# A third weight buffer, and two plain blocks instead of three at the start of three of the four channel mixers

## The chip, the cores and the metric

One core of one Trainium2 chip runs the whole program in one launch. The metric is the device time of that launch in microseconds (us), the median of several runs. A difference of under about 0.3% (5.7 us of 1895) cannot be told from no change.

## The reference

A decoder trunk of two layers on 512 tokens with 1024 channels, all in float32. Each layer adds half a channel mixer, a token mixer and another half channel mixer to the residual `h`:

```python
def swiglu(x, w_gate, w_up, w_down):          # 1024 -> 2816 -> 1024
    return (jax.nn.silu(x @ w_gate) * (x @ w_up)) @ w_down
...
    for i in range(DEPTH):
        h = h + 0.5 * swiglu(rmsnorm(h, ffn_norm_a[i]), ...)
        m = rmsnorm(h, mix_norm[i])
        h = h + (mla_mixer if i % 2 == 0 else nsa_mixer)(m, ...)
        h = h + 0.5 * swiglu(rmsnorm(h, ffn_norm_b[i]), ...)
    return rmsnorm(h, final_norm)
```

The token mixer of layer 0 ("MLA") is latent attention with 16 heads. That of layer 1 ("NSA") has 16 heads in 4 groups and three branches: over compressed blocks, over chosen blocks and over a window.

## The kernel before

The four channel mixers (`ffn`, `idx` 0 to 3) and the two token mixers (`mla`, `nsa`) run in the order ffn 0, mla, ffn 1, ffn 2, nsa, ffn 3. Nothing but their order in the program separates them: a scheduler in the build fixes each engine's instruction order from the code's dependences and its own costs, and each engine then runs its list in order. So work of the next stage is mixed into the end of the one before wherever buffers allow it.

Every matmul of a projection is done three times (high part by high part, high by low, low by high). Each weight slab therefore arrives raw from memory (tile `wr`, two buffers, 512 KB for a block's gate or up weights), ScalarE (ACT) copies its high part into a tile `w`, and VectorE (DVE), or in the attention loops GpSimd (POOL, switched by `lo_pool`), subtracts to get the low part. `wtiles` hands out the `w` tiles in turn from two buffers.

A channel mixer has 22 blocks of 128 hidden channels. Two ways of computing a block's gate and up projections stand beside each other:

- `plain`: 48 matmuls of 256 columns for the gate (`pg`) and 48 for the up projection (`pu`), straight from the normalised input parts `x`. It needs nothing prepared but the weight splits. The first `PLAIN = 3` blocks of every mixer are of this kind.
- seven `product`s of 12 matmuls each (Strassen-Winograd), 84 matmuls, into banks `px`, `pq` and `pg`. They need sums of input parts, made once per mixer by four calls of `combine` (tiles `y`, `u`, `four`), and sums of weight parts, made for every block by `wsums` (tiles `rg` or `wr`, `ru`, `s1`, split into `w`, `wh`, `wl`). Between the products ACT copies a bank that a later product goes on writing (`pg<-px`, `uq<-pq`, `uq<-px`).

While the plain blocks run, the norm's column is made: the last squares are added (`late`, `sumsq`), summed by four small matmuls (`pc`), and twelve small DVE instructions take the reciprocal root (`rsqrt`, tiles `small`). Four more matmuls spread it (`pb`), ACT copies it (`row`), and only then are the plain blocks gated (`tg`, then `tu`, then the parts `ah` and `al` of the activation). In the order that the code gives, `pb` stands between the gate and the up projection of the last plain block. From the fourth block on, down projections of the preceding three blocks (`unit`: eight per three blocks, weights `wdr`, `wd`, bank `pd`) are put behind the products; the last four blocks' down projections come at the end, with weights that used `wslab` and so the `w` tiles.

In `mla`, `query` splits each head's query; the low part is made on POOL (`pool=True`), as is that of each pair's output (`ol`). In `nsa`, the attention loop carries projections of later groups (`pp`, `pv`) in pieces between its tiles, with slabs from `wslab`.

Of the kernel before, what the change touches and what calls it, by code (L numbers as in the profile page):

```python
# [18 lines left out]
P = 128  # L19
S = 512  # L20
D = 1024
KC = D // P
FF = 2816
NF = FF // P
EPS = 1e-6
NEG = -1e30
H = 16
# [19 lines left out]
LASTK = 4  # L47
HS = S // 2
KP = KC // 2
PLAIN = 3  # L50
PAD = 16
TILES = 24
XC = P + 2
NG = 3
# [8 lines left out]
class Kern:  # L63
# [61 lines left out]

    def wtiles(self, kind="x"):

        t = self.first or self.wp.tile([P, 2048 + 3 * PAD], F32R, tag=f"w{self.nw % 2}", name="w")
        self.nw, self.first = self.nw + 1, None
        o, d = {"x": (0, 0), "act": (3 * PAD, 0), "half": (PAD, 2 * PAD)}[kind]  # L130
        return t[:, o : o + 1024], t[:, o + d + 1024 : o + d + 2048]
# [139 lines left out]
            nc.vector.tensor_tensor(t, t, y, op=ALU.mult)  # L271
            nc.vector.scalar_tensor_tensor(y, t, 1.5, y, op0=ALU.add, op1=ALU.mult)

    def norm_col(self, n, s2, pool=False):

        nc = self.nc
        pc = self.bank("o", "pc")
        for i in range(4):
            nc.tensor.matmul(pc[:, i : i + 1], s2[:, i * P : (i + 1) * P], f32v(self.ones)[:, 0:1], start=True, stop=True)
        return self.rsqrt_col(pc[:, 0:4], n, pool)  # L280

    def rsqrt_col(self, s, n, pool=False):
        v, t, col = self.vtc[:, 0:4], self.vtc[:, 4:8], self.vtc[:, 8:12]
# [25 lines left out]
    def wsums(self, idx, f):  # L309


        nc, fp, w_gu = self.nc, self.fp, self.a["w_gu"]
        if f == PLAIN:

            rg = fp.tile([P, 1024], F32, tag="fr", bufs=3, name="rg")
        else:
            rg = self.wp.tile([P, 1024], F32, tag="wr", bufs=2, name="wr")
        nc.sync.dma_start(rg, w_gu[idx, f, 0])
        ru = fp.tile([P, 1024], F32, tag="fr", bufs=3, name="ru")
        nc.sync.dma_start(ru, w_gu[idx, f, 1])  # L320
        s1 = fp.tile([P, S], F32, tag="s1", bufs=1, name="s1")
        g0, g1, u0, u1 = rg[:, :S], rg[:, S:], ru[:, :S], ru[:, S:]

        def split(src, pool, tag, bufs):
            n = src.shape[1]
# [12 lines left out]
        w[1], w[2] = split(rg, self.wp, None, 2)  # L338
        nc.vector.tensor_tensor(s1, u0, u1, op=ALU.add)
        nc.vector.tensor_tensor(u0, u0, g0, op=ALU.add)  # L340
        w[7], w[4] = split(ru, fp, ("fh", "fl"), 3)
        nc.vector.tensor_tensor(g0, g0, s1, op=ALU.add)
        nc.vector.tensor_tensor(g1, g1, g0, op=ALU.add)
        w[6], w[3] = split(rg, fp, ("fh", "fl"), 3)
        w[5], = split(s1, fp, ("sh", "sl"), 2)
        return w
# [22 lines left out]
    def ffn(self, idx, gain_next, ap, tp):  # L369
        nc, a = self.nc, self.a  # L370
        self.scr, self.fp = (tp, "sq", 1), tp
        ah, al, ht, row = {}, {}, [], None
        tg, tu, units = {}, {}, []

        def gate(f, g):

            t = tg[f] = tp.tile([P, S], F32, tag="tg", bufs=2, name="tg")
            nc.vector.tensor_tensor(t, g, row, op=ALU.mult)
            nc.scalar.activation(t, t, AF.Silu, scale=-1.0)
            nc.vector.tensor_tensor(t, t, row, op=ALU.mult)  # L380
# [3 lines left out]

        def act(f):
            t = tu[f]
            if f < PLAIN:
                t = tu_tile()
                nc.vector.scalar_tensor_tensor(t, tu[f], -1.0, tg[f], op0=ALU.mult, op1=ALU.mult)
            else:  # L390
                nc.vector.tensor_tensor(t, t, tg[f], op=ALU.mult)
            ah[f] = ap.tile([P, S], F32R, tag="act", bufs=4 * NG, name="ah")
            al[f] = ap.tile([P, S], F32R, tag="act", bufs=4 * NG, name="al")
            self.split(t, ah[f], al[f])
# [32 lines left out]
                tokens(t)  # L427


        gates = [self.bank("T", "pg") for _ in range(PLAIN)]  # L430
        for f, g in enumerate(gates):
            u = tu[f] = self.bank(("mm", "S")[f % 2], "pu")
            self.plain(idx, f, 0, g)
            if f == 1 and idx == 0:

                squares(0)
                tokens(3)
                squares(1)
            if f == 2:
                pb = self.norm_bcast(col)  # L440
                row = tp.tile([P, S], F32, tag="row", bufs=1, name="row")
                nc.scalar.activation(row, pb, AF.Copy)
                for e in range(2):
                    gate(e, gates[e])
                    act(e)
            self.plain(idx, f, 1, u)
            if f == 0 and idx:
                for c in self.late:
                    self.sumsq(self.h[c])
                col = self.norm_col(D, self.s2)  # L450
            elif f == 1 and idx == 0:
                squares(2)
                squares(3)
                col = self.rsqrt_col(sums, D)
            elif f == 2:
                gate(f, g)
                act(f)
            for p in (((0,), (1,), (2, 3)) if idx else ((0, 1), (2,), (3,)))[f]:
                self.combine(p)
        t = self.tiny  # L460
        for i, g in enumerate(gates[::-1]):
            nc.scalar.activation(t[:, i + 1 : i + 2], g[:, 0:1], AF.Identity, bias=t[:, i : i + 1])

        tail = PLAIN + (NF - 2 - PLAIN) // NG * NG
        for f in range(PLAIN, NF):
            if f % NG == 0 and f <= tail:
                units = [partial(unit, b0=f - NG, c=c) for c in range(KC)]
                left = NG if f < tail else NF - tail
# [36 lines left out]
        self.norm_begin(gain_next)  # L505
        for c in self.order:
            p = self.mm_bank("pd")
            down(p, self.wslab(a["w_down"][idx, c, :, tail * P :], (NF - tail, P), "act"), tail, NF)
            add(c, p)
            self.norm_chunk(c)  # L510

# [130 lines left out]
    def mla(self, gain_next):  # L642
        nc, tc, a = self.nc, self.tc, self.a
        with ExitStack() as cx:
# [106 lines left out]
            def query(h, w=None):  # L751
                p = self.proj(None, P, cqh, cql, "pq", w or query_slab(h))
                t = tp.tile([P, S], F32, tag="tq", bufs=2, name="tq")
                nc.vector.tensor_tensor(t, p, cst, op=ALU.mult)
                qh, ql = self.qtile(), self.qtile()
                self.split(t, qh, ql, pool=True)
                return qh, ql

            qs, oh, ol, o32 = {}, [], [], [None]
# [15 lines left out]
            def end(h):  # L775
# [5 lines left out]
                if h % 2 == 1:  # L781
                    hi = tp.tile([P, S], F32R, tag="o", bufs=12, name="oh")
                    lo = tp.tile([P, S], F32R, tag="o", bufs=12, name="ol")
                    self.split(o32[0], hi, lo, pool=True)
                    oh.append(hi)
                    ol.append(lo)

# [546 lines left out]
```

## Time and profile before

| | |
|---|---|
| median of 3 runs | 1894.92 us (1894.47 to 1899.17) |
| profiled execution | 1895.84 us, of it 1894.1 us from first to last instruction (the span) |
| TensorE (PE) busy | 1865.5 us, 98% |
| VectorE (DVE) busy | 1527.9 us, 81% |
| ScalarE (ACT) busy | 1088.9 us, 57% |
| GpSimd (POOL) busy | 244.7 us, 13%, all but a little of it in the two attention stages |
| HBM | 179.0 MB read, 96 GB/s over the span |

Stages, by the first matmul of each: ffn 0 from 5.7 us, mla from 346.1, ffn 1 from 560.9, ffn 2 from 898.5, nsa from 1235.8, ffn 3 from 1543.1. In the profile, "L165" is line 165 of the kernel before. A matmul's recorded duration overlaps that of its neighbours, so the pace of TensorE is read from the distance of starts, not from durations.

### The profile page before, as it was taken

The numbers are of one execution on the slowest core, as the hardware profiler recorded it, in microseconds if no ns is written. First come the engines' busy times: TensorE is split into PE (matmuls) and PEld (weight loads), VectorE is DVE, ScalarE is ACT, GpSimd is POOL, SyncE is SP. The second block draws the span as 40 slices with busy tenths as digits, with TensorE's granted clock in tenths as the row PEclk, the third lists the DMA queues.
The fourth block names the chain that finished last, engine by engine and source line by source line (L and its number), as shares of the span: only waits on it lengthen the run. The fifth ranks groups of instructions, "written<-read, shape, count | busy, mean of one in ns | idle before, by whom it ended". The sixth has DMA issues, their size and how long they took to land.

```text
span 1894.1 us, 32916 instructions
## 1 busy us (share of the span) xinstructions
PE 1865.5 (98%) x12504; PEld 1695.8 (90%) x12504; DVE 1527.9 (81%) x2913; ACT 1088.9 (57%) x2024; POOL 244.7 (13%) x334
## 2 busy tenths in 40 slices
PE   8999999999999999999999999999989999999998
PEld 8999999878889999998999999888778889999997
DVE  8988886677778888886898878666978988888885
ACT  8555554478765555554654555436867865555553
POOL 0000000047710000000000000015656600000000
PEclk9999999999999999999999999999999999999999
DMA  6433331311132333322333332143121133333321
GB/s 237 131 101 100 102 100 41 112 53 46 60 132 90 124 101 101 102 79 86 130 124 108 105 105 75 55 141 102 51 71 64 43 115 111 111 107 104 104 77 67
DMA packets 75902, 183.26 MB, mean 97 GB/s; under 512 B 9040, under 2 KB 37072, under 8 KB 75744
## 3 DMA queue, kind: packets, MB, share of 16 engines
q1 hardware_dynamic: 72800, 176.39, 29.4%
q10 hardware_dynamic: 2944, 4.77, 0.7%
q8 instruction: 98, 1.61, 0.4%
q14 instruction: 60, 0.49, 0.1%
HBM read 178.96 MB, written 2.16 MB: 96 GB/s over the span
## 4 chain that ended last, share of the span: by engine, by line
PE 86%; DVE 6%; ACT 4%; POOL 2%; issue 1%; DMA 0%; POOLq 0%; SPq 0%; DVEq 0%; ACTq 0%
PE pd L164 8%; PE pd L165 8%; PE pd L163 8%; PE px L353 5%; PE px L354 5%; PE px L355 5%; PE pg L353 4%; PE pg L354 4%; PE pg L355 4%; PE pq L354 3%; PE pq L353 3%; PE pq L355 3%; PE o L1139 1%; PE po L164 1%; PE po L165 1%; PE po L163 1%
## 5 line engine op out<-in xcount | busy, mean ns | idle before, releaser
L164 PE MATMUL pd<-al,wd 128*128 128x512 f32 x576 | 225.3, 391 | 0.0
L163 PE MATMUL pd<-ah,wd 128*128 128x512 f32 x576 | 224.9, 390 | 0.0
L165 PE MATMUL pd<-ah,wd 128*128 128x512 f32 x576 | 224.6, 390 | 0.0
L172 DVE TENSOR_TENSOR w<-wr,w 128x1024 fp32r<-128x1024 f32 x72 | 88.2, 1224 | 123.9 <-ACT w L171 123.9
L353 PE MATMUL px<-four,wh 128*128 128x256 f32 x608 | 168.8, 278 | 0.6 <-ACT pg L478 0.6
L355 PE MATMUL px<-four,wl 128*128 128x256 f32 x608 | 168.0, 276 | 0.0
L354 PE MATMUL px<-four,wh 128*128 128x256 f32 x608 | 167.9, 276 | 0.0
L353 PE MATMUL pq<-four,wh 128*128 128x256 f32 x608 | 167.8, 276 | 0.0
L354 PE MATMUL pq<-four,wh 128*128 128x256 f32 x608 | 167.8, 276 | 0.0
L355 PE MATMUL pq<-four,wl 128*128 128x256 f32 x608 | 167.8, 276 | 0.0
L144 ACT ACTIVATE w<-wr 128x1024 fp32r<-128x1024 f32 (+5 forms) x120 | 100.7, 845 | 113.7 <-issue 25.7
L171 ACT ACTIVATE wd<-wdr 128x384 fp32r<-128x384 f32 x192 | 99.3, 519 | 98.5 <-ACT wd L171 59.1
L402 DVE SCALAR_TENSOR_TENSOR h<-pd,h 128x512 f32<-128x512 f32 x216 | 147.9, 685 | 6.9 <-PE pd L165 6.8
L165 PEld LDWEIGHTS pd<-ah,wd 128*128 128x128 f32 x576 | 108.2, 188 | 22.8
L163 PEld LDWEIGHTS pd<-ah,wd 128*128 128x128 f32 x576 | 108.1, 188 | 20.5
L164 PEld LDWEIGHTS pd<-al,wd 128*128 128x128 f32 x576 | 108.1, 188 | 19.7
L172 DVE TENSOR_TENSOR wd<-wdr,wd 128x384 fp32r<-128x384 f32 x192 | 106.1, 555 | 16.3 <-ACT wd L171 15.6
L146 DVE TENSOR_TENSOR w<-wr,w 128x1024 fp32r<-128x1024 f32 (+4 forms) x81 | 80.7, 998 | 45.1 <-ACT w L144 44.8
L640 ACT ACTIVATE p<-p,small 128x512 f32<-128x512 f32 (+2 forms) x192 | 106.5, 557 | 17.2 <-DVE small L639 14.2
L353 PEld LDWEIGHTS px<-four,wh 128*128 128x128 f32 x608 | 114.1, 188 | 2.5 <-ACT pg L478 1.9
L353 PEld LDWEIGHTS pq<-four,wh 128*128 128x128 f32 x608 | 114.2, 188 | 0.1
L354 PEld LDWEIGHTS pq<-four,wh 128*128 128x128 f32 x608 | 114.1, 188 | 0.1
(354 smaller groups left out, 6106.3 us busy)
## 6 DMA issues: line engine op xcount, KB each, us to landing
wr<-in_w_gu SPq DMA_DIRECT2D x96, 512.0 KB, 3.3
ru<-in_w_gu SPq DMA_DIRECT2D x76, 512.0 KB, 4.2
wdr<-in_w_down SPq DMA_DIRECT2D x192, 192.0 KB, 2.4
wr<-in_w_down SPq DMA_DIRECT2D x24, 256.0 KB, 2.6
wr<-in_mla_w_o SPq DMA_DIRECT2D x8, 512.0 KB, 3.4
wr<-in_nsa_w_q SPq DMA_DIRECT2D x8, 512.0 KB, 3.3
th<-btab_d SPq DMA_DIRECT2D x16, 256.0 KB, 3.5
wr<-in_nsa_w_o SPq DMA_DIRECT2D x8, 512.0 KB, 3.6
```

Source lines behind the costliest of these rows:

```text
L144: self.copied = nc.scalar.activation(wh[:, m], raw[:, m], AF.Copy)
L146: nc.vector.tensor_tensor(wl[:, m], raw[:, m], f32v(wh[:, m]), op=ALU.subtract)
L163: mm(out, wh, xh, start=first, stop=False)
L164: mm(out, wh, xl, start=False, stop=False)
L165: return mm(out, wl, xh, start=False, stop=last)
L171: nc.scalar.activation(hi, src, AF.Copy)
L172: (nc.gpsimd if pool else nc.vector).tensor_tensor(lo, src, f32v(hi), op=ALU.subtract)
L353: mm(out, wh[:, p], xh, start=first and p == 0, stop=False, skip_group_check=True)
L354: mm(out, wh[:, p], xl, start=False, stop=False, skip_group_check=True)
L355: mm(out, wl[:, p], xh, start=False, stop=last and p == KP - 1, skip_group_check=True)
L402: nc.vector.scalar_tensor_tensor(self.h[c], p, 0.5, self.h[c], op0=ALU.mult, op1=ALU.add)
L640: nc.scalar.activation(p_sb[:, :n], p_sb[:, :n], AF.Exp, bias=nm, scale=-1.0, accum_out=sm)
```

## The change

```diff
-PLAIN = 3
+PLAIN = 3, 2, 2, 2
+URGENT = 400
...
-        t = self.first or self.wp.tile(..., tag=f"w{self.nw % 2}", name="w")
+        t = self.first or self.wp.tile(..., tag=f"w{self.nw % 3}", name="w")
...
-    def norm_col(self, n, s2, pool=False):
+    def norm_col(self, n, s2, urgent=0):
...
-        return self.rsqrt_col(pc[:, 0:4], n, pool)
+        with self.tc.high_priority(urgent) if urgent else nullcontext():
+            return self.rsqrt_col(pc[:, 0:4], n)
...
+        def spread():
+            pb = self.norm_bcast(col)
+            nc.scalar.activation(row, pb, AF.Copy)
+            for e in range(plain - 1):
+                gate(e, gates[e])
+                act(e)
...
-        gates = [self.bank("T", "pg") for _ in range(PLAIN)]
+        gates = [self.bank("T", "pg") for _ in range(plain)]
         for f, g in enumerate(gates):
             u = tu[f] = self.bank(("mm", "S")[f % 2], "pu")
             self.plain(idx, f, 0, g)
+            if f == plain - 1:
+                spread()
...
             if f == 0 and idx:
-                for c in self.late:
-                    self.sumsq(self.h[c])
-                col = self.norm_col(D, self.s2)
+                with self.tc.high_priority(URGENT):
+                    for c in self.late:
+                        self.sumsq(self.h[c])
+                col = self.norm_col(D, self.s2, URGENT)
...
-            for p in (((0,), (1,), (2, 3)) if idx else ((0, 1), (2,), (3,)))[f]:
+            for p in (((0, 1), (2, 3)) if plain == 2 else ((0, 1), (2,), (3,)))[f]:
                 self.combine(p)
...
-            down(p, self.wslab(a["w_down"][idx, c, :, tail * P :], (NF - tail, P), "act"), tail, NF)
+            raw = tp.tile([P, D], F32, tag="fr", bufs=3, name="wdr")[:, : (NF - tail) * P]
+            nc.sync.dma_start(raw, a["w_down"][idx, c, :, tail * P :])
+            w = [... for t in self.sum_tiles(1024)]
+            self.split(raw.rearrange("p (k c) -> p k c", c=P), *w)
+            down(p, w, tail, NF)
...
-                self.split(t, qh, ql, pool=True)          # mla, query
+                self.split(t, qh, ql, pool=h > 1)
...
-                    self.split(o32[0], hi, lo, pool=True) # mla, end of a pair of heads
+                    self.split(o32[0], hi, lo, pool=h + 1 < H)
...
-    nc = bacc.Bacc("TRN2", target_bir_lowering=False, num_devices=1)
+    nc = bacc.Bacc("TRN2", target_bir_lowering=False, num_devices=1, dynamic_dma_scratch_size=1024)
```

In words: ffn 1, 2 and 3 start with two plain blocks, so one more block in each is of the seven-product kind; `w` tiles come from three buffers, and room for the third is taken from a DMA scratch area (16384 bytes per partition before, 1024 after; a `w` tile has 8384); the last four blocks' down weights use the sum tiles; three splits of MLA move from POOL to DVE; the norm column's instructions get priority in the scheduler. The column is `pb`'s input, and `pb` now stands inside the up projection of the second plain block.

TensorE at the start of ffn 1, before:

```order
L365 MATMUL pg<-x,w 128x256
L366 MATMUL pg<-x,w 128x256
L367 MATMUL pg<-x,w 128x256
L291 MATMUL pb<-ident,small 128x128 x4
L365 MATMUL pu<-x,w 128x256
L366 MATMUL pu<-x,w 128x256
```

and in the changed kernel, where 21 of the 48 matmuls of `pu` stand ahead of `pb`:

```order
L367 MATMUL pu<-x,w 128x256
L368 MATMUL pu<-x,w 128x256
L369 MATMUL pu<-x,w 128x256
L293 MATMUL pb<-ident,small 128x128 x4
L367 MATMUL pu<-x,w 128x256
L368 MATMUL pu<-x,w 128x256
```

`pb` moved from behind the third block's gate to 69 matmuls behind the start of the second block (in ffn 2 it is 83, in ffn 3 it is 77).

ScalarE in ffn 1, at the first seven-product block, before (the copies between products are `uq<-pq`, `pg<-px`, `uq<-px`):

```order
L171 ACTIVATE w<-wr 128x1024
L171 ACTIVATE ah<-tu 128x512 x2
L379 ACTIVATE tg<-tg 128x512
L462 ACTIVATE gains<-pg,gains 128x1
L480 ACTIVATE uq<-pq 128x256
L462 ACTIVATE gains<-pg,gains 128x1
L478 ACTIVATE pg<-px 128x256
L462 ACTIVATE gains<-pg,gains 128x1
L482 ACTIVATE uq<-px 128x256
```

and in the changed kernel:

```order
L172 ACTIVATE w<-wr 128x1024
L468 ACTIVATE gains<-pg,gains 128x1
L484 ACTIVATE pg<-px 128x256
L486 ACTIVATE uq<-pq 128x256
L172 ACTIVATE ah<-tu 128x512
L488 ACTIVATE uq<-px 128x256
L172 ACTIVATE ah<-tu 128x512
L172 ACTIVATE wh<-s_6814 128x512
L172 ACTIVATE wh<-ru 128x1024
L491 ACTIVATE pg<-px 128x256
```

One `ah` copy of a plain block now stands between two copies of the first seven-product block, and on TensorE no down projection stands among or behind that block's products, as four `pd` matmuls did before.

GpSimd in the attention loop of NSA, with buffer numbers (a name in the changed kernel counts 42 higher than the same tile before; `w_15652` and `w_15658` are the two slabs of `vals`, that is `w_15694` and `w_15700` after), before:

```order
L1091 TENSOR_SCALAR p_15434<-p_15434,small_76,gat_14124 128x512
L1091 TENSOR_SCALAR p_15457<-p_15457,small_76,gat_14124 128x384
L172 TENSOR_TENSOR ohl_15480<-o32_15260,ohl_15479 128x512
L1091 TENSOR_SCALAR p_15489<-p_15489,small_76,gat_14124 128x384
L150 TENSOR_TENSOR w_15652<-wr_15651,w_15652 128x512 x2
L1091 TENSOR_SCALAR p_15508<-p_15508,small_76,gat_14124 128x512
```

and in the changed kernel:

```order
L1101 TENSOR_SCALAR p_15476<-p_15476,small_76,gat_14166 128x512
L1101 TENSOR_SCALAR p_15499<-p_15499,small_76,gat_14166 128x384
L173 TENSOR_TENSOR ohl_15522<-o32_15302,ohl_15521 128x512
L1101 TENSOR_SCALAR p_15531<-p_15531,small_76,gat_14166 128x384
L151 TENSOR_TENSOR w_15700<-wr_15699,w_15700 128x512 x2
L1101 TENSOR_SCALAR p_15550<-p_15550,small_76,gat_14166 128x512
```

The place of the first `vals` slab now holds the second: the low parts of all slabs of the loop stand one slab earlier.

More of the change, by code (lines that the diff above doesn't have):

```diff
@@ L126, in wtiles @@
     def wtiles(self, kind="x"):
-        t = self.first or self.wp.tile([P, 2048 + 3 * PAD], F32R, tag=f"w{self.nw % 2}", name="w")
+        t = self.first or self.wp.tile([P, 2048 + 3 * PAD], F32R, tag=f"w{self.nw % 3}", name="w")
         self.nw, self.first = self.nw + 1, None
@@ L312, in wsums @@
         nc, fp, w_gu = self.nc, self.fp, self.a["w_gu"]
-        if f == PLAIN:
+        if f == PLAIN[idx]:
             rg = fp.tile([P, 1024], F32, tag="fr", bufs=3, name="rg")
@@ L371, in ffn @@
         self.scr, self.fp = (tp, "sq", 1), tp
-        ah, al, ht, row = {}, {}, [], None
+        ah, al, ht, plain = {}, {}, [], PLAIN[idx]
         tg, tu, units = {}, {}, []
@@ L386, in act @@
             t = tu[f]
-            if f < PLAIN:
+            if f < plain:
                 t = tu_tile()
@@ L427, in ffn @@
                 tokens(t)
-        gates = [self.bank("T", "pg") for _ in range(PLAIN)]
+        def spread():
[4 more added lines that the diff above has]
+                act(e)
+        row = tp.tile([P, S], F32, tag="row", bufs=1, name="row")
+        gates = [self.bank("T", "pg") for _ in range(plain)]
         for f, g in enumerate(gates):
@@ L438, in ffn @@
                 squares(1)
[L439 to L445, printed above, removed]
             self.plain(idx, f, 1, u)
             if f == 0 and idx:
-                for c in self.late:
-                    self.sumsq(self.h[c])
-                col = self.norm_col(D, self.s2)
+                with self.tc.high_priority(URGENT):
+                    for c in self.late:
+                        self.sumsq(self.h[c])
+                col = self.norm_col(D, self.s2, URGENT)
             elif f == 1 and idx == 0:
@@ L454, in ffn @@
                 col = self.rsqrt_col(sums, D)
-            elif f == 2:
+            if f == plain - 1:
                 gate(f, g)
                 act(f)
-            for p in (((0,), (1,), (2, 3)) if idx else ((0, 1), (2,), (3,)))[f]:
+            for p in (((0, 1), (2, 3)) if plain == 2 else ((0, 1), (2,), (3,)))[f]:
                 self.combine(p)
@@ L462, in ffn @@
             nc.scalar.activation(t[:, i + 1 : i + 2], g[:, 0:1], AF.Identity, bias=t[:, i : i + 1])
-        tail = PLAIN + (NF - 2 - PLAIN) // NG * NG
-        for f in range(PLAIN, NF):
+        tail, left = (NF - 2) // NG * NG, 1
+        for f in range(plain, NF):
             if f % NG == 0 and f <= tail:
@@ L507, in ffn @@
             p = self.mm_bank("pd")
-            down(p, self.wslab(a["w_down"][idx, c, :, tail * P :], (NF - tail, P), "act"), tail, NF)
+            raw = tp.tile([P, D], F32, tag="fr", bufs=3, name="wdr")[:, : (NF - tail) * P]
+            nc.sync.dma_start(raw, a["w_down"][idx, c, :, tail * P :])
+            w = [t[:, : (NF - tail) * P].rearrange("p (k c) -> p k c", c=P) for t in self.sum_tiles(1024)]
+            self.split(raw.rearrange("p (k c) -> p k c", c=P), *w)
+            down(p, w, tail, NF)
             add(c, p)
```

## The prediction

> **What bounds the kernel now.** I read the page first (busy times, chain), then the stage windows, then TensorE's waits, and then single stretches of the timeline.
>
> ```profile
> span 1894.1 us, 32916 instructions
> PE 1865.5 (98%) x12504; PEld 1695.8 (90%) x12504; DVE 1527.9 (81%) x2913; ACT 1088.9 (57%) x2024; POOL 244.7 (13%) x334
> PE 86%; DVE 6%; ACT 4%; POOL 2%; issue 1%; DMA 0%; POOLq 0%; SPq 0%; DVEq 0%; ACTq 0%
> ```
>
> TensorE (PE) is 98% busy and carries 86% of the chain that ended last. DMA is no part of that chain (0%), so the smaller DMA scratch, of which no row shows a use, is costed at nothing; were transfers to slow down, this share would show it.
>
> The next rows are windows: start and end, length, then busy time and count of PE, PE weight loads, DVE, ACT, POOL, and last the granted clock, DMA share and GB/s. The first is the whole of ffn 1, the second its opening up to about the fourth block.
>
> ```profile
> 560.80:898.50 337.70, 337.48 (x2429) 315.70 (x2429) 279.46 (x437) 180.21 (x291) 0.00 (x0) 1.00 0.32 101
> 560.80:609.90 49.10, 48.91 (x408) 47.73 (x408) 42.48 (x72) 31.71 (x47) 0.00 (x0) 1.00 0.35 117
> ```
>
> PE is without a break at full clock in a channel mixer: 0.22 us idle in 337.70. So a matmul less is time saved, as long as nothing else becomes late. DVE is the nearest rival: 83% over the stage, 42.48/49.10 = 87% in the opening, and the opening is what the change shortens.
>
> PE's waits of 0.2 us or more that the change can touch (engine, line, releaser: total us, times, longest):
>
> ```profile
> PE ptc L1058 <- POOL e L1053: 4.1, 4, 2.4
> PE pv L164 <- POOL w L150: 1.7, 2, 1.0
> PE pg L353 <- ACT pg L485: 1.2, 3, 0.8
> PE px L353 <- ACT pg L478: 0.6, 3, 0.2
> ```
>
> **T1, matmuls out.** Each of ffn 1, 2, 3 has one plain block (96 matmuls) less and one seven-product block (84) more: 12 less each, 36 in all. The first two rows stand half a plain block apart, the last two a whole seven-product block:
>
> ```profile
> 578.13 0.28 PE L365 MATMUL pu<-x,w 128*128 128x256 f32 x1
> 583.57 0.28 PE L365 MATMUL pg<-x,w 128*128 128x256 f32 x1
> 1200.40 0.28 PE L353 MATMUL px<-x,w 128*128 128x256 f32 x1
> 1209.97 0.39 PE L163 MATMUL pd<-ah,wd 128*128 128x512 f32 x1
> ```
>
> 583.57 - 578.13 = 5.44 us for 48 matmuls, 0.1134 each. A plain block is 10.88, a seven-product block 9.57. Per mixer 10.88 - 9.57 = 1.31, for three 3.93; by count 36 x 0.1134 = 4.08. I take -4.0. On DVE and ACT the swap adds work: three DVE sums and four splits in place of two splits, and three bank copies on ACT. That is covered by PE in the middle of a mixer; in the opening it isn't certain (T4).
>
> **T2, the third weight buffer in the NSA loop.** Four waits of PE are for a slab part that was split late, since the slab before held the buffer:
>
> ```profile
> 1306.88 0.50 PE L165 MATMUL pp<-x,w 128*128 128x512 f32 x1 [0.59 <-POOL w L150]
> 1383.30 0.39 PE L163 MATMUL pv<-w,x 128*128 128x256 f32 x1 [0.71 <-ACT w L144]
> 1384.70 0.38 PE L164 MATMUL pv<-w,x 128*128 128x256 f32 x1 [1.02 <-POOL w L150]
> 1386.41 0.58 PE L164 MATMUL pv<-w,x 128*128 128x256 f32 x1 [0.73 <-POOL w L150]
> ```
>
> The sum is 0.59 + 0.71 + 1.02 + 0.73 = 3.05 us. In the changed order the low parts stand a whole slab earlier on POOL, so all four should go; the matmul after a wait can itself be slower (0.58 in the last row, against 0.28 in T1's first), for which I allow 0.15 each, an estimate of half that difference. I take -3.2; the ends are 0 (waits that only move) and -3.7. What is late next is the wait for `e` on POOL (4.1 us in the waits above, 2.4 its longest): it stands behind the same POOL work as before, so I leave it. A raw slab still has only two `wr` buffers, and a transfer can't start earlier than those come free; the split then waits instead of the matmul.
>
> **T3, three splits from POOL to DVE in MLA.** Two waits of PE are for them. Behind the first two rows stand DVE's time for such a split twice, alone and beside a POOL split; then POOL's own pair, beside that DVE one and in two separate instructions.
>
> ```profile
> 402.56 0.50 PE L165 MATMUL s<-four 128*128 128x512 f32 x1 [0.63 <-POOL four L172]
> 543.70 0.50 PE L164 MATMUL po<-ol,w 128*128 128x512 f32 x1 [0.63 <-POOL ol L172]
> 1386.71 0.69 DVE L929 TENSOR_TENSOR four<-t,four 64x512 fp32r<-64x512 f32 x1
> 1383.80 1.40 DVE L929 TENSOR_TENSOR four<-t,four 64x512 fp32r<-64x512 f32 x1 [1.03 <-ACT four L928]
> 1383.39 2.97 POOL L150 TENSOR_TENSOR w<-wr,w 128x512 fp32r<-128x512 f32 x2
> 1407.09 1.30 POOL L150 TENSOR_TENSOR w<-wr,w 128x512 fp32r<-128x512 f32 x1
> ```
>
> POOL takes 1.30 for 512 columns, DVE 0.69: the split is done 0.6 us sooner, just what PE waited (0.63 twice). With both gone, -1.26; I take -1.2. DVE's three extra instructions, 3 x 0.69 = 2.1 us, lie at the edges of MLA, beside PE work. The ends: -1.8 with what a restart costs, and +1.5 if DVE takes 1.40 as in the fourth row (0.71 more at each of two places, late for PE instead).
>
> That fourth row and the POOL pair of 2.97, against 2 x 1.30, ran at the same time, and both are long. The Trainium skill, page "SBUF — State Buffer", section "Who interferes with whom", says that a DVE operation with two inputs in SBUF and a GpSimd one shut each other out for a whole instruction. The trace agrees for this pair; by that rule, with POOL still splitting the next heads, T3 would come out near its upper end (R4 below) instead of at -1.2.
>
> **T4, the openings of ffn 1, 2, 3.** What goes: the waits of the two last rows of PE's waits above, 1.2 + 0.6 = 1.8 us, which lie at first seven-product blocks. What may come: two things.
>
> *The column.* PE runs its list in order, so if the norm's column is not there when PE reaches `pb`, PE stops.
>
> ```profile
> 560.85 0.28 PE L365 MATMUL pg<-x,w 128*128 128x256 f32 x1
> 572.59 0.36 PE L365 MATMUL pg<-x,w 128*128 128x256 f32 x1
> 568.47 0.68 DVE L340 TENSOR_TENSOR ru<-ru,rg 128x512 f32<-128x512 f32 x1
> 569.07 1.22 DVE L146 TENSOR_TENSOR w<-wr,w 128x1024 fp32r<-128x1024 f32 x1
> 570.21 1.22 DVE L172 TENSOR_TENSOR four<-u,four 128x1024 fp32r<-128x1024 f32 x1
> 571.34 0.42 DVE L238 TENSOR_TENSOR u<-y,u 128x256 f32<-128x256 f32 x1
> 571.68 0.68 DVE L237 TENSOR_TENSOR u<-y 128x512 f32<-128x512 f32 x1
> 577.71 0.15 DVE L272 SCALAR_TENSOR_TENSOR small<-small 128x4 f32<-128x4 f32 x1
> 582.83 0.15 DVE L272 SCALAR_TENSOR_TENSOR small<-small 128x4 f32<-128x4 f32 x1
> 589.01 0.49 PE L291 MATMUL pb<-ident,small 128*128 128x128 f32 x3
> ```
>
> The first block with the column's sums takes 572.59 - 560.85 = 11.74 us. In the new order 69 matmuls follow before `pb` in ffn 1, 83 in ffn 2, 77 in ffn 3: PE is there 11.74 + 69 x 0.1134 = 19.6, 21.2 and 20.5 us after the opening's start. Before, the column ended 582.83 + 0.15 - 560.85 = 22.1 after it, and had until 589.01 (28.2). So it must come 2.5 us sooner. DVE's rows ahead of the column's last instruction in the new order of ffn 1 are 9 of 512 columns, 2 slightly longer squares, 7 of 1024, 8 of 256 and 12 tiny ones. By distances of starts above: 9 x 0.60 + 2 x 0.67 + 7 x 1.14 + 8 x 0.34 + 12 x 0.07 = 18.3 us, from about 1.0 after the start: 19.3, against 19.6. (0.67 is an estimate from the 512-column row; 0.07 is half the tiny ones' 0.15, since they overlap.) For ffn 2 and 3 the same count gives 21.5 and 20.8 against 21.2 and 20.5: 0.3 us late each. Both are closer than a hand count can tell; I take +0.6 for the three.
>
> *The gating.* Once spread, the column goes through ACT and DVE before the plain blocks' `ah` is there:
>
> ```profile
> 590.30 0.60 ACT L442 ACTIVATE row<-pb 128x512 f32<-128x512 f32 x1
> 590.91 1.28 ACT L379 ACT_TABLE_LOAD   x1
> 592.21 1.19 ACT L379 ACTIVATE tg<-tg 128x512 f32<-128x512 f32 x2
> 584.92 1.23 DVE L146 TENSOR_TENSOR w<-wr,w 128x1024 fp32r<-128x1024 f32 x1 [1.94 <-ACT w L144]
> 590.30 1.22 DVE L172 TENSOR_TENSOR w<-rg,w 128x1024 fp32r<-128x1024 f32 x1 [4.16 <-ACT w L171]
> 1601.30 0.53 ACT L171 ACTIVATE wd<-wdr 128x384 fp32r<-128x384 f32 x1 [1.70 <-DMA wdr<-in_w_down]
> 1603.10 0.39 PE L353 MATMUL pg<-x,wh 128*128 128x256 f32 x1 [0.79 <-ACT pg L485]
> ```
>
> From PE's 19.6: `pb` and `row` until 21.0, table load until 22.3, the two `tg` until 23.5, then DVE's products on top of its splits, and `tu` at about 28.8 to 29.3. In ACT's new order one `ah` copy, which needs `tu`, stands between the copies `uq<-pq` and `uq<-px`; `uq<-px` is then done at 29.7, and the product that goes on in that bank could start at 28.9. PE waits about 0.8, in each of three openings: +2.4. Before, `pd` matmuls stood there as cover; now none do, so nothing hides it. DVE had 1.94 + 4.16 us idle in the old opening (rows 584.92 and 590.30); the new block's sums and splits eat that. The ends of T4 are -1.8 (no new wait at all) and +4 (the column 0.5 late and the `ah` stall 1.4 in each). Sum: 2.4 + 0.6 - 1.8 = +1.2.
>
> An example of such a chain is in the last two rows: a `wd` copy on ACT waited 1.70 for its transfer, and PE then waited 0.79 for a bank copy that stood behind it and needed nothing of it. [...]
>
> The tail's down weights (sum tiles in place of `w`), PLAIN's effect on the blocks' numbering and the moves of `combine` cost nothing on PE: same matmuls, and DVE has 17% free over the stage (window of ffn 1). Without that cover the tail's DVE split, four parts of 0.60, would cost at most 2.4 per mixer; no row points to that.
>
> **The sum.** -4.0 - 3.2 - 1.2 + 1.2 = -7.2 us. The profiled execution before took 1895.84 (span 1894.1 and 1.7 around it), 0.92 over the median of 1894.92. So 1888.6 for a profiled run, 1887.7 for the median.
>
> **The rivals.**
>
> R1, the openings become DVE-bound: T4 is at +4 and T3 at 0, so the sum is -4.0 - 3.2 + 4 = -3.2, 1891.7, no change that can be measured. For it speaks DVE's 87% in the opening with a block that needs more DVE work; against it that PE loses only the excess over 1 or 2 us there.
>
> R2, the third buffer only moves the waits: the raw slabs have two buffers still, and POOL does its list in order. T2 is about 0: -4.0 - 1.2 + 1.2 = -4.0, 1890.9, no change. For it speaks the `e` row, which shows POOL late in that loop anyway; against it that the parts stand a slab earlier on POOL.
>
> R3, slower: the column stays as late as it was, and each `pb` stops PE. Without T4 the sum is -8.4; to be slower by over 5.7 us the openings have to lose 14.1, or 4.7 each, so the column must come later than 19.6 + 4.7 = 24.3 after the start. Say 25: 3 x 5.4 = 16.2, and 1894.92 - 8.4 + 16.2 = 1902.7. Against it: it came at 22.1 without any priority (2.5 late, 7.5 for three: 1894.0, still no change). For it: twelve dependent instructions on a DVE that has new sums to make, each of which can be put behind a 1.2 us split; in the trace of ffn 1 the last one ended 5 us after an earlier one (rows 577.71 and 582.83).
>
> R4, DVE and POOL stand in each other's way in MLA: T3 is +1.5, as in the 1.40 row. The sum is -4.0 - 3.2 + 1.5 + 1.2 = -4.5, 1890.4, no change. Against it: one such pair in the rows, and the three splits are at the edges of MLA, where POOL has just lost that work.
>
> R5, better: no new wait in the openings, T4 at -1.8, restarts at their best: -4.1 - 3.7 - 1.8 - 1.8 = -11.4, 1883.5.
>
> **How the numbers follow.** Forecast 0.51, R1 0.18, R2 0.14, R3 0.06, R4 0.04, R5 0.07. A difference of 0.3%, 5.7 us, is about what a measurement of this kernel can tell from no change. The forecast's case has about 0.02 on its upper side that lies within it. Faster by more (below 1889.2): 0.49 + 0.07 of R5 + 0.04 of R2 (waits that go in part) = 0.60. Slower: 0.06. The rest, 0.34, is within. The range leaves out R3 and holds the other cases but for their outer parts, since each rests on hand counts: low 1882 (R5 and 1.5 under it), high 1893.5 (R1 with the column 2 us later in one opening).
>
> **What the profile of the changed kernel would show.** T1: windows of ffn 1 and 2 shorter by 1.3 us each, less what their openings wait. T2: no wait for `w` at `pp` and `pv`; if R2, the same microseconds under another tile. T3: the two 0.63 waits gone, no DVE row of 1.4 in their place. T4: `pb` without a wait, and one wait near 0.8 for `uq` on ACT in each opening. I am wrong if `pb` waits for DVE's `small` by more than 2 us in each opening, if the NSA stage keeps its length, or if another engine's name takes over the waits in the opening.

## The result, and the profile after

The changed kernel takes 1913.87 us (median of 4; 1913.42 to 1916.35), the kernel before, measured beside it, 1895.37: ratio 1.0096, 95% interval 1.0079 to 1.0114. It is 18.5 us slower, where 1887.7 was forecast.

From the changed kernel's page (its span is 1912.5 us):

```profile
PE 1888.3 (99%) x12468; PEld 1720.0 (90%) x12468; DVE 1554.5 (81%) x2940; ACT 1080.0 (56%) x2039; POOL 242.0 (13%) x331
```

The 36 matmuls are gone (12504 to 12468), and still TensorE is busy for 22.8 us more. So it does not wait more; its matmuls have become slower. PE's waits in the changed kernel say the same:

```profile
PE pg L367 <- ACT w L145: 5.8, 1, 5.8
PE ptc L1068 <- POOL e L1063: 3.1, 3, 2.4
PE pb L293 <- DVE small L273: 1.4, 3, 0.7
```

The first row is the start of the program and was there before (5.7). The waits for `w` in NSA have gone, `pb` waits 1.4 us in all (0.65 of it in MLA, about 0.4 in the openings of ffn 1 and of ffn 2). By stage (ffn 0, mla, ffn 1 and 2, nsa, ffn 3), first the kernel before, then the changed one:

```profile
5.74:346.13 340.39, 340.12 (x2420) 317.29 (x2421) 285.11 (x445) 188.68 (x306) 0.00 (x0) 1.00 0.36 115
346.13:560.85 214.72, 210.42 (x1105) 176.17 (x1104) 156.84 (x425) 145.49 (x339) 96.30 (x120) 1.00 0.22 70
560.85:1235.83 674.98, 674.57 (x4857) 631.11 (x4856) 559.61 (x876) 358.89 (x580) 2.04 (x6) 1.00 0.32 101
1235.83:1543.06 307.23, 298.62 (x1654) 251.45 (x1653) 240.45 (x687) 209.93 (x493) 146.11 (x206) 0.99 0.24 74
1543.06:1894.05 350.99, 341.76 (x2473) 319.75 (x2471) 284.55 (x478) 182.98 (x303) 0.00 (x0) 1.00 0.32 104
```

```profile
5.80:351.80 346.00, 345.85 (x2420) 323.74 (x2421) 289.67 (x448) 186.61 (x308) 0.00 (x0) 1.00 0.36 117
351.80:567.59 215.79, 211.38 (x1105) 176.33 (x1104) 159.14 (x426) 144.86 (x339) 91.98 (x117) 1.00 0.20 65
567.59:1255.49 687.90, 686.64 (x4833) 643.10 (x4832) 575.96 (x895) 357.93 (x590) 2.09 (x6) 1.00 0.32 101
1255.49:1557.38 301.89, 297.31 (x1654) 251.42 (x1653) 237.56 (x684) 208.19 (x492) 147.76 (x205) 0.99 0.24 74
1557.38:1912.50 355.12, 347.12 (x2461) 325.42 (x2459) 290.81 (x485) 179.47 (x307) 0.00 (x0) 0.99 0.31 100
```

NSA won 5.3 us. All channel mixers lost: ffn 1 and 2 12.9 us with 24 matmuls less, and ffn 0 5.6 us, although it has the same 2420 matmuls as before. The granted clock (third column from the end) is the same to within 0.01, so a lower clock is not the reason. A seven-product block, which took 9.57 us in the prediction, now takes:

```profile
773.07 0.28 PE L355 MATMUL px<-x,w 128*128 128x256 f32 x1
783.05 0.39 PE L164 MATMUL pd<-ah,wd 128*128 128x512 f32 x1
```

783.05 - 773.07 = 9.98 us for 84 matmuls, 118.8 ns instead of 113.9. And within one plain block, gate and up:

```profile
567.59 0.28 PE L367 MATMUL pg<-x,w 128*128 128x256 f32 x1
573.04 0.28 PE L367 MATMUL pu<-x,w 128*128 128x256 f32 x1
578.75 0.39 PE L280 MATMUL pc<-ones,s 128*128 128x1 f32 x3
```

5.45 us for the gate's 48, 5.71 for the up projection's 48 (113.5 and 119.0 ns each): the same matmuls on the same `x`. Only the weights lie in another buffer, the gate's in the second and the up projection's in the third.

The build gives every tile its byte address in a partition. Cut a partition into lines of 128 bytes; an operand begins in the first half of a line (address modulo 128 under 64) or in the second. (A 256-column operand has 1024 bytes and fills whole lines, so only the place where it begins is meant.) A `w` tile has 8384 bytes, which is 65.5 times 128. A third one therefore moves the beginning of all that lies behind it from one half of a line to the other (addresses modulo 128):

| | `x`, `four` | `w` buffers | all behind `w` (sums' `wh`, `wl`; `ah`, `al`, `wd`) |
|---|---|---|---|
| before | 0 mod 128 | 0, 0 | 64 |
| changed | 0 | 0, 0, 64 | 0 |
| changed, 64 bytes more behind `w1` | 0 | 0, 0, 0 | 64 |

The parts of a `w` tile used for a mixer's blocks begin 64 bytes into it (`PAD`). So before, the 256-column matmuls read moving data that begins in the one half, while weights that begin in the other half were loaded. Counted over the built programs, moving data and the weights of the following matmul begin in the same half for 122 of the 7864 matmuls of 256 columns before, for 5940 of 7828 in the changed kernel. For the up projection above they do, since the third `w` buffer begins at 64; for the gate they don't.

### The profile page after: what moved, and what is told of

It is laid out like the page before. It is cut to its first block, busy times and chain, and to the rows that moved or that the text cites. A ratio compares the mean times of both kernels' runs of the same rounds, so it can differ in the third digit from the quotient of the medians.

```text
span 1912.5 us, 32778 instructions
## 1 busy us (share of the span) xinstructions
PE 1888.3 (99%) x12468; PEld 1720.0 (90%) x12468; DVE 1554.5 (81%) x2940; ACT 1080.0 (56%) x2039; POOL 242.0 (13%) x331
## 4 chain that ended last, share of the span: by engine, by line
PE 90%; DVE 4%; ACT 3%; issue 1%; DMA 1%; POOL 1%; POOLq 0%; SPq 0%; DVEq 0%; ACTq 0%
PE pd L165 8%; PE pd L166 8%; PE pd L164 8%; PE px L355 6%; PE px L357 6%; PE px L356 6%; PE pg L355 4%; PE pg L357 4%; PE pg L356 4%; PE pq L357 4%; PE pq L355 4%; PE pq L356 4%; PE po L164 2%; PE o L1149 2%; PE po L165 2%; PE po L166 2%
## 5 line engine op out<-in xcount | busy, mean ns | idle before, releaser
L355 PE MATMUL px<-four,wh 128*128 128x256 f32 x632 | 178.8, 283 | 0.6 <-ACT pg L484 0.6
L357 PE MATMUL px<-four,wl 128*128 128x256 f32 x632 | 178.0, 282 | 0.0
L356 PE MATMUL px<-four,wh 128*128 128x256 f32 x632 | 177.9, 281 | 0.0
L357 PE MATMUL pq<-four,wl 128*128 128x256 f32 x632 | 177.7, 281 | 0.0
L355 PE MATMUL pq<-four,wh 128*128 128x256 f32 x632 | 177.7, 281 | 0.0
L356 PE MATMUL pq<-four,wh 128*128 128x256 f32 x632 | 177.3, 280 | 0.0
L173 DVE TENSOR_TENSOR wl<-s,wh 128x512 fp32r<-128x512 f32 x79 | 54.6, 691 | 135.9 <-ACT wh L172 135.8
L145 ACT ACTIVATE w<-wr 128x1024 fp32r<-128x1024 f32 (+5 forms) x90 | 79.2, 887 | 87.6 <-PE po L166 18.2
L172 ACT ACTIVATE wh<-s 128x512 fp32r<-128x512 f32 x79 | 49.8, 630 | 139.2 <-PE px L356 137.4
L355 PEld LDWEIGHTS px<-four,wh 128*128 128x128 f32 x632 | 119.5, 189 | 1.4 <-ACT pg L484 1.2
L357 PEld LDWEIGHTS px<-four,wl 128*128 128x128 f32 x632 | 119.7, 189 | 0.0
L356 PEld LDWEIGHTS px<-four,wh 128*128 128x128 f32 x632 | 119.3, 189 | 0.0
L355 PEld LDWEIGHTS pq<-four,wh 128*128 128x128 f32 x632 | 119.1, 188 | 0.0
L356 PEld LDWEIGHTS pq<-four,wh 128*128 128x128 f32 x632 | 118.9, 188 | 0.0
```

The costliest lines, as they stand in the source:

```text
L145: self.copied = nc.scalar.activation(wh[:, m], raw[:, m], AF.Copy)
L172: nc.scalar.activation(hi, src, AF.Copy)
L173: (nc.gpsimd if pool else nc.vector).tensor_tensor(lo, src, f32v(hi), op=ALU.subtract)
L355: mm(out, wh[:, p], xh, start=first and p == 0, stop=False, skip_group_check=True)
L356: mm(out, wh[:, p], xl, start=False, stop=False, skip_group_check=True)
L357: mm(out, wl[:, p], xh, start=False, stop=last and p == KP - 1, skip_group_check=True)
```

## The experiments

**1. Addresses alone.** One line: the second `w` buffer is made longer by 64 bytes, or by 128; in the kernel before, by 64. Every engine's instructions and their order stay the same.

```diff
-        t = self.first or self.wp.tile([P, 2048 + 3 * PAD], F32R, tag=f"w{self.nw % 3}", name="w")
+        t = self.first or self.wp.tile([P, 2048 + (4 if self.nw % 3 == 1 else 3) * PAD], F32R, tag=f"w{self.nw % 3}", name="w")
```

> The changed kernel with 64 unused bytes more behind the second weight buffer; all engines run the same instructions in the same order. Theory A: 5940 matmuls of 256 columns go from about 119.2 back to 113.9 or 114.9 ns, so 26 to 31 us less: 1883 to 1888 us. Theory B, and that the smaller DMA scratch slows something: no change, 1914.

> The same with 128 unused bytes more in place of 64: other addresses again, but the same halves of the 128-byte lines as in the changed kernel. Theory A: 1914, no change against the changed kernel. If any shift of the addresses helps (another period than 128 bytes), it comes out near the kernel with 64 bytes more.

> The kernel before with 64 unused bytes more behind its second weight buffer, same instructions in the same order. Theory A: the sums' splits and the down weights change halves, and about 5800 matmuls of 256 columns with them: 26 to 31 us more, 1921 to 1926. Theory B: no change, 1895.

Measured beside each other, with 1897.35 for the kernel before: with 64 bytes more 1889.28 (ratio 0.9959, 0.9944 to 0.9974), with 128 more 1917.63 (1.0109, 1.0092 to 1.0126), and the kernel before with 64 more 1923.70 (1.0137, 1.0122 to 1.0152). The two paddings of the changed kernel are 28.4 us apart and differ by 5940 - 124 = 5816 matmuls of 256 columns in the same half: 4.9 ns each. In the kernel before, 4852 - 122 = 4730 changed to the same half and cost 26.4 us, 5.6 ns each. The slower kernel of each pair also has 397 and 664 more matmuls of 512 columns in opposite halves; by the 6.3 ns that the sweep below shows for those (an estimate), they would be 2.5 of the 28.4 and 4.2 of the 26.4 us. Instructions, transfers and DMA scratch are the same within each pair, so they are not the cause; the addresses are. The kernel with 64 bytes more, called the repaired kernel from here on, is faster than the one before.

**2. The pace by itself.** Groups of equal matmuls with almost nothing else running, only addresses differ.

> The disputed cost by itself; the work of the kernel is left out and its output is zeros. Groups of 96 equal matmuls run with nothing else on the chip; only the byte addresses of the moving data and of the weights change (a: shift of the moving part, b: of the weights, in bytes from a multiple of 128). Theory A (TensorE is slowed when the data that a 256-column matmul reads and the weights that are loaded beside it lie in the same half of their 128-byte lines): a=b=0, a=0 b=128 and a=b=64 take about 119 ns a matmul, a=0 b=64, a=0 b=192 and a=64 b=0 about 113.4; for 512 columns both take about 227 to 232. Theory B (the slower pace comes from other traffic: more splits and transfers beside the matmuls) : all take 113.4 and 226.8, since nothing else runs.

In that sweep's timeline (start, length of the group, tile, count), the pair 0 and 64 (`pe`, then again as `pu`), the pair 0 and 96 (`pf`) and the pair 0 and 0 (`pt`):

```profile
55.49 11.05 PE L39 MATMUL pe<-m,w 128*128 128x256 f32 x96
66.37 11.68 PE L39 MATMUL pf<-m,w 128*128 128x256 f32 x96
278.94 11.67 PE L39 MATMUL pt<-m,w 128*128 128x256 f32 x96
290.45 11.47 PE L39 MATMUL pu<-m,w 128*128 128x256 f32 x96
```

By starts, `pe` took 10.88/96 = 113.3 ns and `pt` 11.51/96 = 119.9. But `pu`, with the addresses of `pe`, was slow too (11.47 against 11.05 us as a group), and so were the other pairs in opposite halves: 0 and 96 (`pf`) 120.1 ns, 0 and 192, 64 and 0, 32 and 64 117.7 to 118.3. Of all groups of 256 columns `pe` alone reached full pace. So the rule as expected was too simple, and the second sweep used the kernel's own triples and three repeats.

> The work of the kernel is left out and its output is zeros. As in the first sweep, but matmuls come in the kernel's own triples (high by high, high by low, low by high), the moving parts lie at multiples of 512 bytes, and each case is run three times in another order, since in the first sweep one and the same pair of addresses (0 and 64) gave 113 ns once and 118 ns once. Theory A: with 256 columns, weights 64 or 192 bytes off a multiple of 128 (pb, pc, pd) take 113.4 ns in each repeat, weights at 0 or 128 (pa, pe, pf) about 119; with 512 columns pm and pq 227, po about 233. If only what ran before decides, the repeats of one case differ as much as the cases.

Of its rows, the first turn of `pb`, the second turn of all cases, and the last turn of `pc`:

```profile
34.53 22.54 PE L42 MATMUL pb<-m,w 128*128 128x256 f32 x190
235.62 21.93 PE L42 MATMUL pb<-m,w 128*128 128x256 f32 x192
257.39 23.20 PE L42 MATMUL pa<-m,w 128*128 128x256 f32 x192
280.43 21.92 PE L42 MATMUL pc<-m,w 128*128 128x256 f32 x192
302.19 22.94 PE L42 MATMUL pf<-m,w 128*128 128x256 f32 x192
324.97 21.93 PE L42 MATMUL pd<-m,w 128*128 128x256 f32 x192
346.73 23.03 PE L42 MATMUL pe<-m,w 128*128 128x256 f32 x192
369.60 22.56 PE L42 MATMUL po<-m,w 128*128 128x512 f32 x96
392.00 21.96 PE L42 MATMUL pm<-m,w 128*128 128x512 f32 x96
413.79 22.48 PE L42 MATMUL pq<-m,w 128*128 128x512 f32 x96
436.11 22.37 PE L42 MATMUL pn<-m,w 128*128 128x512 f32 x96
570.57 22.77 PE L42 MATMUL pc<-m,w 128*128 128x256 f32 x192
```

With 256 columns, weights 64 bytes off (`pb`) take 21.77/192 = 113.4 ns a matmul, and 64 for the high, 192 for the low part (`pd`) the same; weights at 0 (`pa`) take 120.0, at 128 (`pf`) 118.6. No group with both in the same half reached 113.4, in any turn. In opposite halves `pd` did in all three turns, `pb` in two and `pc` (192 bytes off) in one; in the others they took 117.8 (for `pb` the first turn, 22.54 us for 190; for `pc` the first and the last, 22.77 for 192). So the expected 113.4 in each turn was wrong for `pb` and `pc`: in these runs no group reached full pace without opposite halves, but they were not enough by themselves. What else decides isn't shown; the cases are the same and only their place in the sequence differs. In the kernel the blocks with opposite halves ran at 113.4 to 113.9 ns. With 512 columns it is the other way round: the same address (`pm`) 21.79/96 = 227.0, 64 off (`po`) 233.3, and 128 off (`pq`) 232.5. The expectation of 227 for `pq` was wrong.

**3. The parts of the change, each undone in the repaired kernel.** The results of 3 and 4 are in one table behind 4.

> The changed kernel with two weight buffers instead of three; without the third, the addresses behind fall into the halves that they had in the kernel before, without a pad. If the third buffer is worth the NSA waits (T2 of the prediction, 3.2 us) and nothing else: 3.2 us above the changed kernel with 64 bytes more, about 1892.5 when that one is 1889.3. Rival: with the third buffer ScalarE's copies of new slabs stand earlier and wait for their transfers with the bank copies behind them (six waits of PE for `pg`, 4 us in the profile of that kernel); then two buffers lose 3.2 in NSA and win 3 to 4 there, and the time is the same, 1888.5 to 1889.5.

> The changed kernel with 64 bytes more, but three plain blocks in every mixer. If the 36 matmuls of 0.1134 us are saved at the cost of the three waits for the column in its profile (1.0 us together): 3 us more, 1892.3 when the other is 1889.3. If the openings give all of it back: no difference.

> The changed kernel with 64 bytes more and a third buffer for raw slabs. If transfers start late because the raw buffers are taken, the waits of PE for bank copies behind a late slab go: 3 to 4 us less, 1885.5 to 1886.5 when the other is 1889.3. If the transfers are late for another reason (the queue's order, other transfers): no change.

> The changed kernel with 64 bytes more, and MLA's three splits back on GpSimd. If T3 of the prediction holds, the two waits of 0.63 us return: 1.2 us more, about 1890 when the other is 1888.7 to 1889.3. Rival: in the profile of that kernel PE waits 1.6 us in MLA for DVE's `small` ahead of `s` and 1.8 for the column ahead of `pb`, 0.2 each before; if DVE's three extra splits are their cause, the time falls by 1 to 2 us, to 1887 to 1888.

> The kernel with 64 bytes more and a third raw buffer, with MLA's three splits on GpSimd as in the kernel before. If the splits on DVE win 1.2 us: about 1888.8 when the other is 1887.6. If they cost 1 to 2: 1886 to 1886.6, the fastest so far.

> The changed kernel with 64 bytes more, without the priority for the column's instructions. If the priority is what brings the column in time (T4 of the prediction), `pb` waits 1 to 2.5 us longer in each of the three openings: 3 to 7.5 us more, 1892 to 1896. If the order on DVE gives it early anyway: no difference.

**4. The parts alone, put into the kernel before, and the whole again.**

> The kernel before with one part of the change: the third weight buffer (padded by 64 bytes, with the small DMA scratch). If the parts add up as T2 was forecast: 3.2 us less than before. If as it measured when undone: 5 to 6 less. If the copies of slabs that wait earlier on ScalarE cost something by themselves: less than 3 less.

> The kernel before with one part of the change: MLA's three splits on DVE. T3 of the prediction: 1.2 us less than before. As measured when undone: 4 to 5 less. If they pay only together with the third buffer: no difference.

> The changed kernel with two weight buffers and MLA's splits on GpSimd, so the two plain blocks, the column's priority and the last down weights' new tiles alone. T1 and T4 of the prediction: 2.8 us less than before; as measured when undone, 2 to 3.6 less; if the openings or the new tiles eat it: no difference.

> The changed kernel with 64 bytes more, once more, beside its parts. If its parts add up: their sum below before, 10 to 12 us. If they overlap or cost something together: 7 to 9 us below before again.

Each ratio is to the kernel before as measured beside that row. Its median was 1895.5 to 1897.8, so the ratios are to be compared, not the microseconds.

| kernel | us, median | ratio to before | 95% interval |
|---|---|---|---|
| repaired (64 bytes more), again | 1888.58 | 0.9950 | 0.9938 to 0.9962 |
| two `w` buffers | 1894.85 | 0.9991 | 0.9982 to 1.0000 |
| three plain blocks | 1892.32 | 0.9970 | 0.9958 to 0.9981 |
| third raw buffer | 1887.61 | 0.9947 | 0.9934 to 0.9959 |
| MLA splits on POOL | 1891.56 | 0.9979 | 0.9970 to 0.9987 |
| third raw buffer, MLA splits on POOL | 1891.03 | 0.9973 | 0.9962 to 0.9984 |
| no priority for the column | 1888.80 | 0.9964 | 0.9951 to 0.9976 |
| alone: third buffer | 1891.37 | 0.9966 | 0.9954 to 0.9977 |
| alone: MLA splits on DVE | 1895.78 | 0.9991 | 0.9983 to 1.0000 |
| alone: two plain blocks | 1895.99 | 0.9994 | 0.9985 to 1.0004 |

The whole, run again, gains 9.5 us (7 to 12); the parts alone 6.4, 1.7 and 1.1, together 9.3. So the parts put in alone add up, to within intervals of about 2 us each. Undone, they show more: 0.0041 (third buffer), 0.0029 (MLA) and 0.0020 (plain blocks) against 0.9950, which is 7.8, 5.5 and 3.8 us; against the 0.9959 that the repaired kernel had in part 1 each is 1.7 less. The third buffer and MLA's splits belong together, as the next rows show. A third raw buffer and the column's priority make no difference that these intervals can tell.

Three plain blocks came out as expected (1892.3), and so did the two that make no difference. The third buffer alone (6.4) and MLA's splits alone (1.7) come near one of their cases. The others were missed: two `w` buffers cost more than the 3.2 us or nothing expected; MLA's splits on POOL cost more than 1.2, also with a third raw buffer (0.0026, 4.9 us), where a gain was the rival; the two plain blocks alone gained 1.1 instead of 2.8, which can't be told from nothing; the whole, 9.5, lies between its two cases.

The stages of the repaired kernel, run again, in the same order as above (its profiled execution took 1888.99 us):

```profile
6.01:348.36 342.35, 340.12 (x2420) 317.63 (x2421) 288.79 (x448) 186.81 (x308) 0.00 (x0) 1.00 0.37 118
348.36:564.07 215.71, 210.08 (x1106) 176.33 (x1104) 159.83 (x426) 144.78 (x339) 92.28 (x117) 1.00 0.21 65
564.07:1238.94 674.87, 672.76 (x4833) 629.19 (x4832) 574.87 (x895) 357.10 (x590) 2.09 (x6) 1.00 0.33 103
1238.94:1538.99 300.05, 295.64 (x1653) 250.10 (x1652) 237.31 (x684) 208.00 (x492) 148.23 (x205) 1.00 0.24 75
1538.99:1887.20 348.21, 339.90 (x2461) 318.44 (x2459) 289.80 (x485) 180.06 (x307) 0.00 (x0) 0.99 0.32 102
```

Against the kernel before: ffn 0 2.0 us longer, MLA 1.0 longer, ffn 1 and 2 0.1 shorter, NSA 7.2 and ffn 3 2.8 shorter. (The repaired kernel's other profiled execution has 2.2 and 1.0 longer, 1.0 longer, 5.7 and 2.0 shorter.) In the profile of the kernel before with the third buffer alone, MLA and NSA are:

```profile
348.50:566.04 217.54, 211.56 (x1105) 177.85 (x1104) 157.78 (x426) 146.22 (x341) 95.17 (x120) 0.99 0.22 69
1241.67:1543.42 301.75, 297.18 (x1654) 251.38 (x1653) 239.26 (x687) 209.18 (x494) 148.64 (x206) 0.99 0.25 78
```

It wins 5.5 us in NSA, and loses 2.8 in MLA and 2.3 in ffn 0 (342.68 us). (This profiled execution took 1895.26 us, 3.9 over its kernel's median, so its stages are compared and not its total.) In MLA, the row of TensorE and those of POOL ahead of it, with the third buffer alone:

```profile
403.81 2.51 POOL L150 TENSOR_TENSOR w<-wr,w 128x512 fp32r<-128x512 f32 x2 [3.30 <-ACT w L144]
406.28 1.26 POOL L172 TENSOR_TENSOR four<-tq,four 128x512 fp32r<-128x512 f32 x1
407.60 0.67 PE L165 MATMUL s<-four 128*128 128x512 f32 x2 [2.21 <-POOL four L172]
```

With a free `w` buffer the next slab's split is put ahead of the first head's split on POOL (before, the head's began at 401.23 and the slab's at 405.23), and PE waits 2.21 us for the latter, where it waited 0.63. Moved to DVE, that split has nothing ahead of it on POOL, and the wait goes. But it then runs beside POOL's slab split. In the repaired kernel:

```profile
399.36 1.01 POOL L151 TENSOR_TENSOR w<-wr,w 128x384 fp32r<-128x384 f32 x1 [0.23 <-DVE small L272]
399.38 1.01 DVE L273 SCALAR_TENSOR_TENSOR small<-small 128x4 f32<-128x4 f32 x1
400.54 1.13 PE L293 MATMUL pb<-ident,small 128*128 128x128 f32 x8 [1.83 <-DVE small L273]
404.47 2.99 POOL L151 TENSOR_TENSOR w<-wr,w 128x512 fp32r<-128x512 f32 x2 [4.09 <-ACT w L145]
404.94 1.37 DVE L173 TENSOR_TENSOR four<-tq,four 128x512 fp32r<-128x512 f32 x1 [0.52 <-ACT four L172]
406.24 1.77 DVE L173 TENSOR_TENSOR four<-tq,q 128x512 fp32r<-128x512 f32 x1
```

The two DVE splits take 1.37 and 1.77 us, where each takes 0.69 in the kernel with this part alone, in which POOL's pair begins only after them. Two instructions of MLA's column take 0.94 (at 398.20) and 1.01 instead of 0.16, each beside a POOL split; before, POOL's split began as the column ended. PE's wait for `pb` in MLA is 1.83 us where it was 0.24, and its waits at `s` for DVE's `small` are 1.6 where they were 0.2. So in MLA this part removes one cost of the third buffer, while others stay, and the stage ends 1.0 us longer than before.

In ffn 0, with the third buffer alone, a transfer came late:

```profile
27.16 1.06 ACT L423 ACTIVATE xt<-xt 128x1024 f32<-128x1024 f32 x1 [3.62 <-DMA xt<-in_x_tok]
32.23 0.39 PE L367 MATMUL pg<-x,w 128*128 128x256 f32 x1 [1.19 <-DVE w L146]
48.01 0.38 ACT L478 ACTIVATE pg<-px 128x256 f32<-128x256 f32 x1
48.44 0.39 PE L353 MATMUL px<-four,wh 128*128 128x256 f32 x1 [1.64 <-ACT pg L478]
```

ScalarE waited 3.62 us for the last `xt`, which began at 23.36 before, and what follows in order on ScalarE and DVE came later too: PE waits 1.19 us for a slab's low part and 1.64 for the bank copy `pg<-px`. The changed kernel has a third buffer too, and in its profile `xt` is not late (23.20) and ffn 0 has no such waits. In the repaired kernel `xt` waited 1.5 and 2.8 us in the two executions; with two buffers, in two of the kernels, 0.4 and 0.6. Why the transfer is late, and whether the third buffer has a part in it, is not shown.

The stage of MLA with the splits on DVE alone, which is T3 by itself:

```profile
346.85:560.37 213.52, 210.17 (x1105) 176.01 (x1104) 158.35 (x428) 145.14 (x339) 92.15 (x117) 1.00 0.23 71
```

213.52 against 214.72: 1.20 us less.

In the repaired kernel `pb` waits 0.4, 0.4 and 0.2 us in the openings of ffn 1, 2 and 3. Its longest wait for a bank copy in these mixers, 0.9, lies at the end of ffn 1, where ScalarE's copy of the next mixer's slab waits for its transfer with the bank copy behind it:

```profile
858.99 1.06 ACT L145 ACTIVATE w<-wr 128x1024 fp32r<-128x1024 f32 x1 [3.14 <-DMA wr<-in_w_gu]
860.38 0.39 PE L355 MATMUL pg<-x,wh 128*128 128x256 f32 x1 [0.86 <-ACT pg L491]
```

## Why the prediction was wrong

**The step that failed** is the price of a matmul in T1, and with it the sentence that a matmul less is time saved as long as nothing else becomes late. 0.1134 us was read from rows where moving data and weights begin in opposite halves of their 128-byte lines, and was then taken for all matmuls of the changed kernel. T2 took the third buffer for 8384 bytes of room and a wait less; that it shifts the addresses of all that lies behind it had no term. The missing term is the 28.4 us between the two paddings (4.9 ns for each of 5816 matmuls); less the 7.8 or 9.5 that the repaired kernel gains, it gives 20.6 or 18.9, where 18.5 was measured (interval 15 to 22). The addresses stand in the build of the changed kernel, and the trace of before had rows of the slow pace, the last 256-column matmuls of the program, whose moving data and weights begin in the same half:

```profile
1882.97 0.28 PE L542 MATMUL pd<-w,ah 128*128 128x256 f32 x1
1885.68 0.28 PE L544 MATMUL pd<-wh,al 128*128 128x256 f32 x1
```

23 steps in 1885.68 - 1882.97 = 2.71 us, 117.8 ns each.

**None of the rivals** was it. R3 had the right side, but its mechanism, the column that comes late at `pb`, cost 0.4 us an opening at most. R4's mechanism did come, in MLA: DVE's two splits took 1.37 and 1.77 us there beside POOL's, as above (in the changed kernel 1.37 and 1.78). R4 priced this at +1.5 in place of -1.2; MLA came out 1.1 us longer in the changed kernel, against the 18.5 that the program lost.

**T1 and T4** (-4.0 and +1.2, together -2.8) agree with the repaired kernel as far as its spread allows: three plain blocks cost 2.1 to 3.8 us more there (ratio 0.9970 against 0.9959 and 0.9950), and ffn 1 to 3 together are 2.9 and 1.0 us shorter in its two profiles. The waits for the column are 0.4, 0.4 and 0.2 against 0, 0.3 and 0.3. The priority of the column makes no difference that could be measured. The stall of 0.8 in each opening did not come in the repaired kernel; instead single bank copies are late elsewhere (0.9 and 0.5 us, at the ends of ffn 1 and 2). In the two plain blocks alone, with two `w` buffers, PE waits 1.50 us for such a copy in the opening of ffn 1 (589.48) and 1.33 in ffn 3 (1589.64), and 4.7 us in all of ffn 1 to 3 where it waited 1.5. So T4 was about +3.2 there, which fits the gain of 1.1 from 36 matmuls less. The 1.8 us that T4 counted as going were misread: 0.24 lie in ffn 0, and 0.95 behind the first seven-product block of ffn 3; only 0.6 stood at first seven-product blocks of ffn 1 to 3.

**T2** (-3.2) was under-sized in NSA, where the stage is 5.3 us shorter in the changed kernel, 5.5 with the third buffer alone, 5.7 and 7.2 in the repaired one. The waits named went; the wait for `e`, which was left in the sum, fell by 1.0 too (4.1 to 3.1); why the stage gains 1.2 us and more beyond that is not shown. The term left out that with a free buffer POOL's slab splits come earlier in MLA: 2.8 us lost there without the DVE splits.

**T3** (-1.2) was right alone: MLA's stage is 1.20 us shorter in the profile, though the program's 1.7 us can hardly be told from nothing. Beside the third buffer the splits' own time was mis-sized, 1.37 and 1.77 us instead of 0.69, and MLA is 1.0 us longer than before instead of 1.2 shorter. Taking the splits back costs 3.8 to 5.5 us by the medians; the wait of 2.2 us at `s` returns with it, but the stage of MLA is only 0.7 us longer (216.37), so most of that cost is not traced.

**The sum** of -7.2 is close to what the repaired kernel gained, 7.8 and 9.5 when measured twice, but that is luck: T1 to T4 say -1.2 for MLA, -2.8 for ffn 1 to 3, -3.2 for NSA and nothing for ffn 0, and its stages have +1.0, -2.9, -7.2 and +2.0. NSA gained more than twice its term and paid for two stages that became longer. The pace of what doesn't wait was never put to the question.

## What to carry to other kernels

When a change adds, drops or resizes a buffer, take the new address of each tile that TensorE reads, and compare moving data and weights modulo 128 bytes before and after; a buffer of 8384 bytes, no multiple of 128, cost 28 us here, and a pad of 64 bytes brought them back. When a TensorE-bound stage changes length without waits, look at the distance of starts within one block before looking for a reason in other engines. A buffer more lets a scheduler move work earlier on in-order engines, so ask what it then stands ahead of, and what it then runs beside. When a sum comes out right, compare it stage by stage before trusting its terms.

## What the runs showed of the hardware

TensorE's pace depended on where its two operands begin. With 256 columns, 113.4 ns a matmul at best with the weights 64 bytes off, 118 to 120 with both in the same half of 128-byte lines; with 512 columns 227 at the same address, 231 to 233 at 64 or 128 bytes off. The Trainium skill, page "SBUF — State Buffer", section "Who interferes with whom", gives TensorE separate read ports for the moving operand and for the weights and says that it never waits on anyone. Here nothing ran beside the matmuls of a group but one DVE copy of 0.4 us, and operands of TensorE itself that begin in the same half made a matmul 6% longer (120.0 against 113.4); the measurement decides. What lies behind it, and why the same addresses (`pb` and `pc`, `pe` and `pu`) took either pace, the runs don't show.

A DVE instruction that ran beside a POOL split took longer: splits of 512 columns 1.37 and 1.77 us instead of 0.69, and tiny instructions of the column 0.94 and 1.01 instead of 0.16.
